# Average pooling over 2x2x2 windows: all loads contiguous and, but for the first, paired, twelve of them for ten, and two stores for three

## The chip, the cores and the metric

One core of one Trainium2 chip. The time is the device time of one execution in microseconds (us). A KB is 1024 bytes; "a load of 24 KB" has 24 KB in each of 128 partitions, so 3 MiB.

## The reference

```python
x: (8, 32, 32, 32, 32) float32, kernel_size = 2
result[:, :, i, j, k] = mean(x[:, :, 2*i:2*i+2, 2*j:2*j+2, 2*k:2*k+2])   # (8, 32, 16, 16, 16)
```

It reads 32 MiB and writes 4 MiB. The 256 pairs of batch and channel are 256 rows of 128 KB. Any piece that holds whole pairs of planes (8 KB a pair) can be pooled by itself, so a partition may take a piece of its own row, or all partitions together one contiguous stretch.

## The kernel before

The first half of the input is read with one row per partition, pieces 128 KB apart; the second half in contiguous stretches.

```python
KF = 256                                   # 1 KB of float32
xv = x.rearrange("b c d h w -> (b c) (d h w)")[:P]              # first half
xf = x.rearrange("b c d h w -> (b c d h w)")[P * 128 * KF:]     # second half
plan = [(0, 0, 32), (0, 32, 32), (0, 64, 32), (0, 96, 32),
        (1, 0, 24), (1, 24, 24), (1, 48, 24), (1, 72, 24), (1, 96, 16), (1, 112, 16)]
for t, k, kb in plan:
    tin = pool_in.tile([P, 32 * KF], F32, tag="tin", name="tin")      # 5 buffers
    buf = tin[:, :kb * KF]
    src = xv[:, k*KF:(k+kb)*KF] if t == 0 else xf[P*k*KF:P*(k+kb)*KF].rearrange("(p e) -> p e", p=P)
    nc.sync.dma_start(out=buf, in_=src)
    pool_unit(buf, t, k, kb, split=k == 96 and t == 1)   # add planes, add columns, add rows and scale
# stores: contiguous part 1 (3 KB runs), the whole first half (16 KB runs), contiguous part 2 (2 KB runs)
... (cut) ...
# on the built program: a contiguous load reads two rows at once
elif "in_" in src.memref and ap[0][0] == row:
    ap = [[2 * row, 64], [1, 2 * row]]
... (cut) ...
# the first load is moved ahead of the opening barrier; the end waits for the stores alone
```

Per unit the vector engine (DVE) makes two adds and a third that also scales; each of the three counts one on its semaphore. All transfers are issued by the queue of SyncE (SPq).

## Time and profile before

| | before |
|---|---|
| time, median | 91.38 us (91.28 to 91.54, 6 runs) |
| span of the profile | 86.7 us |
| DMA queue's share of 16 engines | 99.2% |
| DVE busy | 64.5 us |
| loads land (from vector starts and issues) | 12.0, then every 9.7, 7.30 and 4.9; the last at 80.1 |
| last store lands | 89.9 us |

The lines that carry this are shown in the prediction. Each is read for its releaser: a vector instruction that waited for a transfer starts as that transfer lands.

### The profile page before, as it was taken

The numbers are of one execution on the slowest core, as the hardware profiler recorded it, in microseconds if no ns is written. First come the engines' busy times: TensorE is split into PE (matmuls) and PEld (weight loads), VectorE is DVE, ScalarE is ACT, GpSimd is POOL, SyncE is SP. The second block draws the span as 40 slices with busy tenths as digits, with TensorE's granted clock in tenths as the row PEclk, the third lists the DMA queues.
The fourth block names the chain that finished last, engine by engine and source line by source line (L and its number), as shares of the span: only waits on it lengthen the run. The fifth ranks groups of instructions, "written<-read, shape, count | busy, mean of one in ns | idle before, by whom it ended". The sixth has DMA issues, their size and how long they took to land.

```text
span 86.7 us, 91 instructions
## 1 busy us (share of the span) xinstructions
DVE 64.5 (74%) x41; POOL 0.2 (0%) x4
## 2 busy tenths in 40 slices
DVE  0000049992999649992999999799599959999992
POOL 0000000000000000000000000000000000000000
DMA  8969998899988999699888988889988899889999
GB/s 242 469 287 454 484 484 378 363 469 484 484 363 363 484 484 484 287 439 605 363 363 386 703 363 363 363 363 658 431 363 363 363 484 484 363 363 424 414 463 401
DMA packets 1297, 36.72 MB, mean 424 GB/s; under 512 B 176, under 2 KB 176, under 8 KB 176
## 3 DMA queue, kind: packets, MB, share of 16 engines
q1 hardware_dynamic: 1297, 36.72, 99.2%
HBM read 33.55 MB, written 4.19 MB: 436 GB/s over the span
## 4 chain that ended last, share of the span: by engine, by line
DMA 70%; DVE 26%; issue 0%; SPq 0%; DVEq 0%
DMA tin<-in_x_dram 70%; DVE tin L68 14%; DVE tin L71 8%; DVE obuf L74 4%; SPq L87 0%; DVE dummy L74 0%; DVEq L105 0%
## 5 line engine op out<-in xcount | busy, mean ns | idle before, releaser
L68 DVE TENSOR_TENSOR tin<-tin 128x4096 f32<-128x4096 f32 (+3 forms) x11 | 35.9, 3260 | 19.9 <-DMA tin<-in_x_dram 19.9
L71 DVE TENSOR_TENSOR tin<-tin 128x2048 f32<-128x2048 f32 (+2 forms) x10 | 18.6, 1865 | 0.3
L74 DVE CUSTOM_DVE_ANT_1 obuf<-tin 128x1024 f32<-128x1024 f32 (+2 forms) x10 | 10.1, 1011 | 0.3
L74 DVE DVE_READ_ACCUMULATOR2_ANT dummy<- 128x1 f32 x10 | 0.8, 82 | 0.0
L210 POOL MEMSET const-bfloat16-1.0<- 128x1 bf16 x1 | 0.1, 102 | 0.0
L210 POOL MEMSET const-uint8-127<- 128x1 uint8 x1 | 0.1, 102 | 0.0
L210 POOL MEMSET const-float32-0.0<- 128x1 f32 x1 | 0.1, 99 | 0.2 <-issue 0.2
L210 POOL MEMSET const-float32-1.0<- 128x1 f32 x1 | 0.1, 99 | 0.0
## 6 DMA issues: line engine op xcount, KB each, us to landing
tin<-in_x_dram SPq DMA_DIRECT2D x4, 4096.0 KB, 25.5
tin<-in_x_dram SPq DMA_DIRECT2D x4, 3072.0 KB, 34.5
tin<-in_x_dram SPq DMA_DIRECT2D x2, 2048.0 KB, 25.5
out_dram<-obuf SPq DMA_DIRECT2D x1, 2048.0 KB, 10.3
out_dram<-obuf SPq DMA_DIRECT2D x1, 1536.0 KB, 6.2
out_dram<-obuf SPq DMA_DIRECT2D x1, 512.0 KB, 4.8
```

Source lines behind the costliest of these rows:

```text
L68: nc.vector.tensor_add(out=bv[:, o0:o1], in0=a[:, o0:o1, 0], in1=a[:, o0:o1, 1])
L71: nc.vector.tensor_add(out=c, in0=bv[:, :, 0], in1=bv[:, :, 1])
L74: nc.vector.tensor_tensor_reduce(out=obuf[t][:, o0:o0 + od * 256].rearrange("p (j k) -> p j k", k=16), in0=cv[:, :, 0], in1=cv[:, :, 1], s ...
L210: nc = _bacc.Bacc("TRN2", target_bir_lowering=False, num_devices=1)
```

## The change

Its intent: one uniform layout, with every load contiguous and, from the second on, paired, that is, read as 64 rows of double length; sizes that let the vector engine keep up; two stores instead of three, of which the first is held until shortly before the loads end.

```diff
-    pool_in = ... bufs=5          # of 32 KB
+    pool_in = ... bufs=6          # of 24 KB
-    plan = [(0, 0, 32), ... (1, 112, 16)]
+    plan = [24] * 8 + [16] * 4
-        src = xv[...] if t == 0 else xf[...]
+        nc.sync.dma_start(out=buf, in_=xf[P*k*KF:P*(k+kb)*KF].rearrange("(p e) -> p e", p=P))
-    for k, n, kb in [(0, 4, 3), (12, 2, 2)]: ... and the whole first half after the first
+    for k, n, kb in [(0, 8, 3), (24, 4, 2)]:
...
+    plain = next(i for i in program if isinstance(i, mybir.InstDMACopy))    # the first load stays unpaired
-        elif "in_" in src.memref and ap[0][0] == row:
+        elif "in_" in src.memref:
             ap = [[2 * row, 64], [1, 2 * row]]
...
-        copy.replace(w, wait_value=w.wait_value + 1) if w.ant_name.startswith("DVE") else w
+        copy.replace(w, wait_value=31) if w.ant_name.startswith("DVE") else w
```

More of the change, by code (lines that the diff above doesn't have):

```diff
@@ L27, in pool_rows, with pool_unit @@
     add = mybir.AluOpType.add
-    xv = x.rearrange("b c d h w -> (b c) (d h w)")[:P]
-    ov = out.rearrange("b c d h w -> (b c) (d h w)")[:P]
-    xf = x.rearrange("b c d h w -> (b c d h w)")[P * 128 * KF:]
-    of = out.rearrange("b c d h w -> (b c d h w)")[P * 16 * KF:]
-    pool_in = ctx.enter_context(tc.tile_pool(name="pin", bufs=5))
+    xf = x.rearrange("b c d h w -> (b c d h w)")
+    of = out.rearrange("b c d h w -> (b c d h w)")
+    pool_in = ctx.enter_context(tc.tile_pool(name="pin", bufs=6))
     pool_out = ctx.enter_context(tc.tile_pool(name="pout", bufs=1))
-    obuf = [pool_out.tile([P, 16 * KF], F32, name=f"obuf{t}") for t in range(2)]
+    obuf = pool_out.tile([P, 32 * KF], F32, name="obuf")
     dummy = pool_out.tile([P, 1], F32, name="dummy")
-    plan = [
-        (0, 0, 32),
-        (0, 32, 32),
-        (0, 64, 32),
-        (0, 96, 32),
-        (1, 0, 24),
-        (1, 24, 24),
-        (1, 48, 24),
-        (1, 72, 24),
-        (1, 96, 16),
-        (1, 112, 16),
-    ]
-    def pool_unit(buf, t, k0, kb, split):
+    plan = [24] * 8 + [16] * 4
+    def pool_unit(buf, k0, kb):
         od = kb // 8
@@ L64, in pool_unit @@
         b = buf[:, :od * 1024]
-        bv = b.rearrange("p (o e) -> p o e", o=od)
-        cuts = (0, 1, od) if split else (0, od)
-        for o0, o1 in zip(cuts, cuts[1:]):
-            nc.vector.tensor_add(out=bv[:, o0:o1], in0=a[:, o0:o1, 0], in1=a[:, o0:o1, 1])
+        nc.vector.tensor_add(
+            out=b.rearrange("p (o e) -> p o e", o=od), in0=a[:, :, 0], in1=a[:, :, 1])
         bv = b.rearrange("p (e ww) -> p e ww", ww=2)
@@ L74, in pool_unit @@
         nc.vector.tensor_tensor_reduce(
-            out=obuf[t][:, o0:o0 + od * 256].rearrange("p (j k) -> p j k", k=16),
+            out=obuf[:, o0:o0 + od * 256].rearrange("p (j k) -> p j k", k=16),
             in0=cv[:, :, 0], in1=cv[:, :, 1],
@@ L78, in pool_unit @@
         )
-    for t, k, kb in plan:
-        tin = pool_in.tile([P, 32 * KF], F32, tag="tin", name="tin")
+    k = 0
+    for kb in plan:
+        tin = pool_in.tile([P, 24 * KF], F32, tag="tin", name="tin")
         buf = tin[:, :kb * KF]
-        if t == 0:
-            src = xv[:, k * KF:(k + kb) * KF]
-        else:
-            src = xf[P * k * KF:P * (k + kb) * KF].rearrange("(p e) -> p e", p=P)
-        nc.sync.dma_start(out=buf, in_=src)
-        pool_unit(buf, t, k, kb, split=k == 96 and t == 1)
-    for k, n, kb in [(0, 4, 3), (12, 2, 2)]:
+        nc.sync.dma_start(
+            out=buf, in_=xf[P * k * KF:P * (k + kb) * KF].rearrange("(p e) -> p e", p=P))
+        pool_unit(buf, k, kb)
+        k += kb
+    for k, n, kb in [(0, 8, 3), (24, 4, 2)]:
         nc.sync.dma_start(
             out=of[P * k * KF:P * (k + n * kb) * KF].rearrange("(u p e) -> p u e", u=n, p=P),
-            in_=obuf[1][:, k * KF:(k + n * kb) * KF].rearrange("p (u e) -> p u e", u=n),
+            in_=obuf[:, k * KF:(k + n * kb) * KF].rearrange("p (u e) -> p u e", u=n),
         )
-        if k == 0:
-            nc.sync.dma_start(out=ov, in_=obuf[0])
 def kernel(tc: tile.TileContext, x: bass.AP, kernel_size: int, out: bass.AP):
@@ L107 @@
     program = blocks[tc.starting_block_idx].instructions
+    plain = next(i for i in program if isinstance(i, mybir.InstDMACopy))
     for n, i in enumerate(program):
-        if not isinstance(i, mybir.InstDMACopy):
+        if not isinstance(i, mybir.InstDMACopy) or i is plain:
             continue
```

## The prediction

> **What bounds the kernel now.** I read the page's head, then the DMA queue line, then the timeline of the vector engine (DVE) and of the queue that issues transfers (SPq), and last the chain, because here the chain misleads.
>
> ```profile
> span 86.7 us, 91 instructions
> DVE 64.5 (74%) x41; POOL 0.2 (0%) x4
> ...
> q1 hardware_dynamic: 1297, 36.72, 99.2%
> HBM read 33.55 MB, written 4.19 MB: 436 GB/s over the span
> ...
> DMA 70%; DVE 26%; issue 0%; SPq 0%; DVEq 0%
> ...
> out_dram<-obuf SPq DMA_DIRECT2D x1, 2048.0 KB, 10.3
> out_dram<-obuf SPq DMA_DIRECT2D x1, 1536.0 KB, 6.2
> out_dram<-obuf SPq DMA_DIRECT2D x1, 512.0 KB, 4.8
> ```
>
> The packets of one queue fill 99.2% of sixteen transfer engines' span: they are never without work. The vector engine is busy 74% and has its rests. The chain gives it 26% all the same, because the span ends with the last instruction, the issue of the last store at 85.11, and not with that store's landing; before that issue stands the vector work on the last load. But the landing is what the time waits for. From the next view, the three stores were issued at 77.66, 78.33 and 85.11; with the medians above they landed at 77.66 + 6.2 = 83.9, 78.33 + 10.3 = 88.6 and 85.11 + 4.8 = 89.9. So the last store was in the queue 3.5 us before the one ahead of it was through. The end is 89.9 in the trace's clock, and the time of 91.35 is 1.45 more, outside what the trace shows; I carry it over unchanged.
>
> ```profile
> 12.01 4.42 DVE L68 TENSOR_TENSOR tin<-tin 128x4096 f32<-128x4096 f32 x1 [12.01 <-DMA tin<-in_x_dram]
> ...
> 21.70 4.42 DVE L68 TENSOR_TENSOR tin<-tin 128x4096 f32<-128x4096 f32 x1 [1.67 <-DMA tin<-in_x_dram]
> ...
> 31.42 4.43 DVE L68 TENSOR_TENSOR tin<-tin 128x4096 f32<-128x4096 f32 x1 [1.71 <-DMA tin<-in_x_dram]
> ...
> 55.74 3.36 DVE L68 TENSOR_TENSOR tin<-tin 128x3072 f32<-128x3072 f32 x1 [0.53 <-DMA tin<-in_x_dram]
> ...
> 63.04 3.36 DVE L68 TENSOR_TENSOR tin<-tin 128x3072 f32<-128x3072 f32 x1 [1.15 <-DMA tin<-in_x_dram]
> ...
> 70.34 3.36 DVE L68 TENSOR_TENSOR tin<-tin 128x3072 f32<-128x3072 f32 x1 [1.15 <-DMA tin<-in_x_dram]
> ...
> 76.41 2.48 DVE L68 TENSOR_TENSOR tin<-tin 128x1024 f32<-128x1024 f32 x2
> 77.66 0.62 SPq L93 DMA_DIRECT2D out_dram<-obuf  x1
> 78.33 0.58 SPq L98 DMA_DIRECT2D out_dram<-obuf  x1
> ...
> 85.11 0.57 SPq L93 DMA_DIRECT2D out_dram<-obuf  x1
> ```
>
> A row that ends with a DMA as releaser starts as its load lands, so these starts are a clock of the loads. Loads of 32 KB a partition (4 MiB, one row read at a time, rows of the tensor 128 KB apart) land every 9.7 us; loads of 24 KB (3 MiB, contiguous, two rows in one read) every 7.30. The two 16 KB loads were issued at 49.17 and 55.24 and took 26.0 and 24.9 to land: at 75.2 and 80.1, so 4.9 each. The steps are 9.71 - 7.30 = 2.41 and 7.30 - 4.90 = 2.40: **a load costs 0.08 us and 2.405 us per MiB**, whether contiguous and paired or neither. The first began 12.01 - 9.71 = 2.30 us after the start. The stores follow the same line: from 80.1 to 89.9 is 9.8 us for 4 MiB in three, and 4 x 2.405 + 3 x 0.08 = 9.86.
>
> **What the Trainium skill says.** "DMA: Bandwidth & Descriptors", Specifications, gives a fabric ceiling of 435 GB/s for the sixteen engines' way into SBUF. The trace agrees: 2.405 us per MiB is 436 GB/s. "HBM Reference", Specifications, says that a core streaming alone measures about 425 GB/s, bounded by its engines; agreed, 4.194 MB in 9.71 us is 432. The same DMA page, Latency and other measured facts, reports that a row pitch of 512 KiB or more lowers the rate (207 GB/s at 512 KiB). The old first half has a pitch of 128 KiB, which the page doesn't list, and its loads ran at 432 GB/s against 431 for the contiguous ones: there is no such loss to win back here. And its Queues, rings and completion order says that an engine consumes descriptors in ring order; agreed: the first store was issued at 77.66 yet landed 3.8 us after the last load, about what its own bytes take (1.5 x 2.405 = 3.6).
>
> **The change, part by part.**
>
> Loads. Bytes are the same, 32 MiB. Four of 32, four of 24 and two of 16 KB become eight of 24 and four of 16. Old sum: 2.30 + 4 x 9.71 + 4 x 7.30 + 2 x 4.90 = 80.14, which the trace confirms (80.1). New: 2.30 + 8 x 7.30 + 4 x 4.90 = 80.30. That is +0.16, two more loads at 0.08. Contiguity and pairing get nothing, since the two kinds already lie on one line. The first load stays unpaired and comes before the opening barrier as before, so the 2.30 stays.
>
> Buffers. Six of 24 KB in place of five, mixed. Load 7 waits for unit 1 to be worked off, at about 9.6 + 6.1 = 15.7, while five loads still queue behind unit 1 until 2.30 + 6 x 7.30 = 46.1. The last load waits for unit 6, at about 46.1 + 6.1 = 52.2, and its turn comes at 75.4. The queue stays fed.
>
> Vector work. A 24 KB unit takes 76.41 - 70.34 = 6.07 us, a 16 KB unit 4.20 (80.80 to 85.00 in the timeline). Twelve units: 8 x 6.07 + 4 x 4.20 = 65.4 busy against 64.5. All of it lies beside transfers, as 6.07 < 7.30 and 4.20 < 4.90. Near the end: unit 8 lands at 2.30 + 58.4 = 60.7 and is done at 66.8; unit 9 runs to 71.0, unit 10 to 75.2; unit 11 lands at 75.4, its first add (2.29 us) ends at 77.7; unit 12 lands at 80.3 and is done at 84.5.
>
> First store, 24 KB a partition (3 MiB). It now waits for vector count 31. Each unit counts three; the old wait of 24 + 1 was for the first add of unit 9, which the trace confirms (77.66 is where the first of the two short adds from 76.41 ends). So 31 is the first add of unit 11, 77.7: 2.6 us ahead of the loads' end, against 80.1 - 77.66 = 2.4 before, where the engines didn't run dry. It moves from 80.3 to about 80.30 + 3 x 2.405 + 0.08 = 87.6.
>
> Second store, 8 KB (1 MiB). Issued at about 84.5, still 3.1 us before the one ahead of it is through; of these the issue takes 0.6 and the way to the first byte about 1.2 (the chain shows the first load's transfer from 1.18 after its issue at 0). So it hides. Both stores: 4 x 2.405 + 2 x 0.08 = 9.78; the same sum lay 0.06 above the old measurement, so 9.7 to 9.8. Two MiB now go out in runs of 2 and 3 KB in place of 16 KB; the old store with 3 KB runs kept the line (3.8 measured, 3.7 by the sum), so I charge nothing.
>
> Sum: 80.30 + 9.75 = 90.05, and 1.45 after it: **91.5 us**, +0.15 on 91.35.
>
> **The rivals.**
> 1. Contiguous, paired reads are faster, and the half that gets them pays. For it: longer reads mean fewer packets. Against: 7.30 lies on the line through 9.71 and 4.90 to 0.01 us. Even 1% on 16 MiB would be 0.4 us: 91.1.
> 2. The second store becomes a new wait. One long store behind one short one leaves fewer transfers in the queue. If the last store missed its place by 1 us the time were 92.5. Against: 3.1 us of lead, and the store ahead of it is 3 MiB rather than 2.
> 3. The first store leaves a hole at 80.3. It has 8 runs a partition to describe, in place of 4; issues took 0.62 us with four and 0.57 with two, so some 0.73 with eight. A lead of 2.6 should take that; if not, some tenths.
> 4. Short runs to memory are slow. If the 2 MiB that move from 16 KB runs to 2 and 3 KB lost 5%, that were 0.24 us: 91.75.
>
> **Range and chances.** The sum of small terms is +0.15. Repeats spread by 0.11 us; rivals 3 and 4 could add 0.3, rival 1 take 0.3 away. So 91.5, with 91.15 to 91.95. For 2% either way the time must reach 89.5 or 93.2. The first needs an end at 88.1, which is less than the bytes take at the shown rate (2.30 + 36 x 2.405 = 88.9); the second needs a hole of 1.7 us, which only rival 2 or 3 in full could make.
>
> **What the changed profile would show.** Loads landing every 7.30 and then 4.90 us, the last at 80.3, say that the line holds; 7.2 or less would be rival 1. The first store issued at 77.7 and landing at 87.6 says that it kept its place; a later landing is rival 3 or 4. The second issued near 84.5 and landing at 90.0. DVE near 65.4. The span should fall to about 86.1, as the last issue comes 0.6 earlier, though the time does not: the chain will still name vector work that decides nothing. The prediction is wrong if the DMA share falls well below 99%, or if the time outside the trace isn't 1.45 again.

## The result, and the profile after

| | before | after |
|---|---|---|
| time, median | 91.38 us (91.28 to 91.54) | 92.27 us (92.09 to 92.45), 6 runs each |
| ratio | | 1.0097, 95% interval 1.0080 to 1.0114 |

Ratios are the mean time of one kernel's fast runs over that of the other's of the same rounds, so not quite the ratio of the medians. The change costs 0.9 us: within 2%, but six times the 0.15 us forecast, and outside the range.

From the page of the changed kernel: head, DMA queue, chain, and the stores' issues with their us to landing.

```profile
span 86.9 us, 100 instructions
DVE 65.4 (75%) x48; POOL 0.2 (0%) x4
...
q1 hardware_dynamic: 1151, 36.68, 99.0%
...
DMA 82%; DVE 12%; SPq 3%; issue 0%; DVEq 0%
...
out_dram<-obuf SPq DMA_DIRECT2D x1, 3072.0 KB, 10.0
out_dram<-obuf SPq DMA_DIRECT2D x1, 1024.0 KB, 5.5
```

The vector engine's time is what the sum said, 65.4. The queue's share looks healthy. The timeline of the changed kernel shows where the time went:

```profile
10.39 3.36 DVE L50 TENSOR_TENSOR tin<-tin 128x3072 f32<-128x3072 f32 x1 [10.39 <-DMA tin<-in_x_dram]
...
17.68 3.36 DVE L50 TENSOR_TENSOR tin<-tin 128x3072 f32<-128x3072 f32 x1 [1.13 <-DMA tin<-in_x_dram]
...
61.51 3.36 DVE L50 TENSOR_TENSOR tin<-tin 128x3072 f32<-128x3072 f32 x1 [1.15 <-DMA tin<-in_x_dram]
...
78.51 7.43 SPq L75 DMA_DIRECT2D out_dram<-obuf  x2
...
81.06 2.29 DVE L50 TENSOR_TENSOR tin<-tin 128x2048 f32<-128x2048 f32 x1 [0.59 <-DMA tin<-in_x_dram]
```

The first load lands at 10.39 where 9.60 was forecast. From there all is as forecast: 7.29 to the second, (61.51 - 17.68) / 6 = 7.305 for each of the next six, and (81.06 - 61.51) / 4 = 4.89 for each of the last four. The loads end at 81.06 rather than 80.30; the delay of the first 10 us is carried to the end.

**What the completion records add.** The Trainium skill, "DMA: Bandwidth & Descriptors", Why a DMA increments its semaphore by 16 and not by 1, says that each transfer engine adds one when its own share has landed. The trace agrees: every load has sixteen marks, and the load is usable at the last. So one can see how even the engines are. The median mark is here the ninth of the sixteen:

```
                         last mark   median mark   last minus median
before, first load         11.99        11.86            0.13
before, last load          80.11        79.97            0.14
after,  first load         10.37         9.54            0.83
after,  last load          81.04        80.22            0.82
```

Before, a load of 24 KB in first place would have had its median mark at 11.86 - 2.41 = 9.45; after, it is at 9.54. So most engines are nearly as early as before and **one is far behind** (the second-last mark is at 9.92). A packet is what one engine reads at once, here one row of the load. The packet records show the late one: the sixteen first packets (32 KB) of the kernel before end between 2.80 and 3.18 us; those of the changed one (24 KB) end between 2.38 and 3.20, but for one that took 2.38 us, where the median took 1.59, and ended at 3.65. After that its packets take 0.91 to 0.93 as all others do. The marks of the first and the last load show the same distance: no load makes the lag up. In the last store it is still 0.63.

In the profiled runs (92.31 against 91.29) the last store lands at 90.92 against 89.90, and the time outside the trace is 1.39 in both. The 1.02 divides into the first load, 10.37 - (11.99 - 2.41) = 0.79; the other loads, (81.04 - 10.37) - (80.11 - 11.99 + 2.405) = 0.15; and the stores, (90.92 - 81.04) - (89.90 - 80.11) = 9.88 - 9.79 = 0.09.

### The profile page after: what moved, and what is told of

Read it like the earlier page. It is cut to its first block, busy times and chain, and to the rows that moved or that the text cites. A ratio compares the mean times of both kernels' runs of the same rounds, so it can differ in the third digit from the quotient of the medians.

```text
span 86.9 us, 100 instructions
## 1 busy us (share of the span) xinstructions
DVE 65.4 (75%) x48; POOL 0.2 (0%) x4
## 4 chain that ended last, share of the span: by engine, by line
DMA 82%; DVE 12%; SPq 3%; issue 0%; DVEq 0%
DMA tin<-in_x_dram 82%; DVE tin L50 7%; DVE tin L54 3%; SPq L67 3%; DVE obuf L57 2%; DVE dummy L57 0%; DVEq L85 0%
## 5 line engine op out<-in xcount | busy, mean ns | idle before, releaser
L50 DVE TENSOR_TENSOR tin<-tin 128x3072 f32<-128x3072 f32 (+1 forms) x12 | 36.0, 3002 | 19.2 <-DMA tin<-in_x_dram 19.0
L54 DVE TENSOR_TENSOR tin<-tin 128x1536 f32<-128x1536 f32 (+1 forms) x12 | 19.0, 1580 | 0.4
L57 DVE CUSTOM_DVE_ANT_1 obuf<-tin 128x768 f32<-128x768 f32 (+1 forms) x12 | 10.4, 869 | 0.4
```

The source lines that it names most:

```text
L50: nc.vector.tensor_add(out=b.rearrange("p (o e) -> p o e", o=od), in0=a[:, :, 0], in1=a[:, :, 1])
L54: nc.vector.tensor_add(out=c, in0=bv[:, :, 0], in1=bv[:, :, 1])
L57: nc.vector.tensor_tensor_reduce(out=obuf[:, o0:o0 + od * 256].rearrange("p (j k) -> p j k", k=16), in0=cv[:, :, 0], in1=cv[:, :, 1], scal ...
```

## The experiments

Each was timed beside the kernel before. "Lag" is the last mark of the first load less the median mark. It and the landings are of the one profiled run of each kernel; the times are of four to six runs. Eighteen kernels were run, in five groups.

### Group 1: pairing, the form of the issue, or the sizes?

The first theory was that the paired loads queued in the first 2 us, which take longer to issue, hold up an engine's first packet. The rivals: the first load's size, or its contiguous layout.

**Six loads unpaired.** `plain` holds the first six loads instead of one:

```diff
-    plain = next(i for i in program if isinstance(i, mybir.InstDMACopy))
+    plain = [i for i in program if isinstance(i, mybir.InstDMACopy)][:6]
```

> The changed kernel with its first six loads (those issued at the start) reading one row at a time, as only its first did; loads 7 to 12 stay paired. Theory P (the paired loads that are issued in the first 2 us hold up one engine's first packet, and that engine stays behind to the end): the first load lands at about 9.6 instead of 10.37, the landing spread of its 16 engines falls from 1.2 to about 0.35 us, the time is about 91.5. Theory S (a first load of 24 KB rows starts worse than one of 32 KB): still 10.3 and 92.3. Theory C (the contiguous layout of the first load starts worse than the 128 KB pitch): still 10.3 and 92.3.

Measured: 92.18 us, ratio 1.0090 (1.0075 to 1.0105), first landing 10.17, lag 0.61.

**All twelve unpaired** (`[:12]`).

> The changed kernel with all twelve loads reading one row at a time. Theory P: as the run with six plain loads, 91.5; should pairing of the later loads be worth something, that run is the faster of the two. Theories S and C: 92.3.

Measured: 92.28 us, ratio 1.0088 (1.0076 to 1.0100), first landing 10.37, lag 0.83. The theory falls: with no pairing anywhere the loss is whole. Nor is pairing worth anything later.

**Six unpaired, but with the long issue form** (the same, and for loads 2 to 6 also `ant_dge_precooked=False`).

> As the run with six plain loads, but loads 2 to 6 take the longer issue (without the sequencer's short form, which the paired ones also lack; some 0.56 us an issue instead of 0.33 to 0.47). If theory P holds because of the issue form and not of the pairing: 92.3 and a first landing at 10.3. If because of the paired reads themselves: 91.5 and 9.6.

Measured: 92.18 us, ratio 1.0086 (1.0073 to 1.0099), first landing 10.10, lag 0.49. The form of the issue does nothing either.

**Old sizes, contiguous.** `plan = [32] * 4 + [24] * 4 + [16] * 2`, five buffers of 32 KB, four unpaired loads, the split add of the kernel before and three stores (runs of 3, 4 and 2 KB, where that kernel had 3, 16 and 2).

> The changed kernel's contiguous layout with the load sizes of the kernel before (four of 32, four of 24, two of 16 KB), its first four loads unpaired, the others paired as before, its split first add and its three stores. Theory P and theory S: first load lands at 12.0 as before, time 91.4. Theory C: it lands near 12.8, time 92.2.

Measured: 91.60 us, ratio 1.0026 (1.0012 to 1.0039), first landing 12.26, lag 0.32. Most of the loss is gone with 32 KB, though all is contiguous; the lag is still over twice the 0.13 of the kernel before. At this point size looked like the cause.

### Group 2: size of the first load, or distance between its rows?

**First load of 32 KB, then eight of 24 and two of 16**, contiguous, in a buffer of its own; three stores.

> Pairing is out: with all loads unpaired the first load still landed at 10.37. The changed kernel with a first load of 32 KB rows (contiguous, unpaired), then eight of 24 and two of 16 KB, a split add and three stores. Theory F (the rows of the very first load alone decide how far the slowest engine falls behind): first landing 12.0 to 12.3 as with the old sizes, last engine at most 0.35 us after the median one, time 91.5 to 91.7. Theory Q (that the queue behind it is made of 24 KB rows, or holds six loads, decides): last engine 0.5 to 0.8 us after the median, first landing 12.5 to 12.8, time 92.0 to 92.3.

Measured: 91.73 us, ratio 1.0044 (1.0031 to 1.0057), first landing 12.27, lag 0.25. The first load decides most of it, not the queue behind it.

**First load of 16 KB** (`[16] + [24] * 8 + [16] * 3`), in a buffer of its own; three stores.

> The same with a first load of 16 KB rows, eight of 24, three of 16 KB. Theory F with size as cause (shorter first rows leave the slowest engine further behind): last engine over 0.8 us behind the median one, time 92.3 to 92.7. If only rows that are not a power of two (24 KB) are bad: last engine at most 0.35 us behind, time 91.6 to 91.8.

Measured: 92.24 us, ratio 1.0103 (1.0088 to 1.0118), first landing 8.01, lag 0.68. That lag lies between the two expectations; the time is just short of the size theory's range.

**The kernel before with 24 KB rows.** The first half in 24, 24, 24, 24 and 32 KB, still 128 KB apart:

```diff
-        (0, 0, 32), (0, 32, 32), (0, 64, 32), (0, 96, 32),
+        (0, 0, 24), (0, 24, 24), (0, 48, 24), (0, 72, 24), (0, 96, 32),
```

> The kernel before with its first half read in four loads of 24 KB and one of 32 KB a partition, rows still 128 KB apart: one more load, 0.08 us. Size as cause: last engine 0.5 to 0.8 us behind the median, first landing 10.1 to 10.4, time 92.0 to 92.3. Pitch between the rows as cause (the contiguous layout is what hurts): last engine 0.15 to 0.3 behind, first landing 9.6 to 9.75, time 91.5.

Measured: 91.36 us, ratio 1.0000 (0.9988 to 1.0012), first landing 9.62, lag 0.17. Its timeline, beside that of the changed kernel above:

```profile
9.64 3.36 DVE L69 TENSOR_TENSOR tin<-tin 128x3072 f32<-128x3072 f32 x1 [9.64 <-DMA tin<-in_x_dram]
...
16.92 3.36 DVE L69 TENSOR_TENSOR tin<-tin 128x3072 f32<-128x3072 f32 x1 [1.13 <-DMA tin<-in_x_dram]
```

Loads of the same size as the changed kernel's land 0.75 earlier, and the time is that of the kernel before. **So size is not the cause.** Where the rows lie remains; group 3 tests it on the first load alone.

**First load paired too**, so that it reads 48 KB at once (`or i is plain` taken out).

> The changed kernel with its first load paired too, so that the first packets read 48 KB. Size of the first packet as cause: last engine at most 0.3 us behind the median; the longer issue costs up to 0.2 us; time 91.6 to 91.8. Layout as cause: 0.5 to 0.8 behind, time 92.3 to 92.5.

Measured: 92.43 us, ratio 1.0128 (1.0110 to 1.0145), first landing 10.47, lag 0.45. The longer issue starts its packets at 1.36 instead of 1.02, and the lag stays high, though just under the 0.5 that was expected of the layout: longer packets don't mend it.

### Group 3: the first load alone, and a version to beat both

Here the first load takes its rows from elsewhere, so a part of the result is wrong on purpose. Bytes, sizes, order and stores stay.

**Changed kernel, first load's rows 128 KB apart:**

```diff
-            out=buf, in_=xf[P * k * KF:P * (k + kb) * KF].rearrange("(p e) -> p e", p=P))
+            out=buf, in_=(
+                xf[:P * 128 * KF].rearrange("(p e) -> p e", p=P)[:, :kb * KF] if k == 0 else
+                xf[P * k * KF:P * (k + kb) * KF].rearrange("(p e) -> p e", p=P)))
```

> The changed kernel, but its first load alone takes its 24 KB rows 128 KB apart instead of back to back (results wrong on purpose in that part; bytes, sizes and all else as they are). Theory C1 (the layout of the very first load decides how far the slowest engine is left behind): last engine 0.1 to 0.3 us behind the median one, first landing 9.6 to 9.75, time 91.5 to 91.6. Rival (the contiguous loads queued behind it matter too): 0.5 or more behind, time 92.0 or more.

Measured: 91.63 us, ratio 1.0025 (1.0013 to 1.0037), lag 0.12.

```profile
9.57 3.36 DVE L50 TENSOR_TENSOR tin<-tin 128x3072 f32<-128x3072 f32 x1 [9.57 <-DMA tin<-in_x_dram]
...
80.25 2.29 DVE L50 TENSOR_TENSOR tin<-tin 128x2048 f32<-128x2048 f32 x1 [0.60 <-DMA tin<-in_x_dram]
```

This one edit brings the first landing to 9.57 and the last to 80.25; the forecast had 9.60 and 80.30. In ratios it takes back 1.0097 - 1.0025 = 0.72%, about 0.66 of the 0.89 us. What stays is 0.25% or 0.23 us (0.12 to 0.34). It is of the size of the 0.15 that was forecast, but not all of that kind: in the profiled runs the loads end 80.23 - 80.11 = 0.12 later than in the kernel before, and the stores take 90.23 - 80.23 = 10.00 for its 9.79.

**Rows 48 KB apart** (48 for 128 in that edit).

> The same with rows 48 KB apart (results wrong on purpose). If the lag falls steadily with the distance (back to back 24 KB: 0.5 to 0.8; 32 KB: 0.25 to 0.3; 128 KB: 0.15): last engine 0.2 to 0.3 behind, time 91.6 to 91.8. If only a wide or a power-of-two distance helps: 0.5 or more, time 92.0 or more.

Measured: 92.32 us, ratio 1.0099 (1.0086 to 1.0112), first landing 10.38, lag 0.74. Twice the distance, no gain at all: the lag doesn't fall steadily.

**Kernel before, first load's 32 KB rows back to back** (and kept unpaired).

> The kernel before, but its first load alone takes its 32 KB rows back to back (results wrong on purpose in that part). Theory C1: last engine 0.25 to 0.35 behind the median one as in the two runs with a contiguous 32 KB first load, first landing 12.2 to 12.3, time 91.5 to 91.7. Rival (contiguous loads behind the first matter): 0.13 behind as before, time 91.35.

Measured: 91.62 us, ratio 1.0019 (1.0007 to 1.0030), first landing 12.21, lag 0.33. The reverse test: contiguous rows in the first load alone cost the kernel before 0.2 us.

**Eight loads, all rows 128 KB apart** (48, 48, 32, 40, 32, 24, 16, 16 KB; three stores; correct).

> A version that should beat both: all rows 128 KB apart, eight loads of 48, 48, 32, 40, 32, 24, 16, 16 KB instead of ten, three stores, correct results. Two loads fewer at 0.08 us: 91.2, ratio 0.998, if the last engine stays within 0.2 us of the median one. If lag grows with size or a store comes late: 91.4 or more.

Measured: 92.11 us (91.93 to 93.15), ratio 1.0093 (1.0056 to 1.0130), lag 0.43. A miss. In the profiled run, one of the longer ones (92.81), beside the lag, the last load lands 81.66 - 75.46 = 6.2 us after the one ahead of it instead of 4.9; packets of 16 KB that take 0.61 elsewhere took up to 1.68 there. Its first store had been issued at 71.79, while the loads still ran.

### Group 4: which distance, and the version again

**Rows of 24 KB, 32 KB apart.**

> The changed kernel with the 24 KB rows of its first load alone 32 KB apart (results wrong on purpose). Theory T (a distance that is a power of two keeps the sixteen engines even): last engine 0.15 to 0.35 us behind the median one, time 91.6 to 91.8. Theory W (only a wide distance does): 0.5 or more behind, time 92.1 or more.

Measured: 91.77 us, ratio 1.0047 (1.0034 to 1.0061), lag 0.20.

**64 KB apart.**

> The same, 64 KB apart (results wrong on purpose). Theory T: 0.1 to 0.3 behind, 91.6 to 91.7. Theory W, with the limit somewhere above 48 KB: anything between 91.6 and 92.2, worse than at 120 KB.

Measured: 91.57 us, ratio 1.0024 (1.0010 to 1.0039), lag 0.13.

**120 KB apart.**

> The same, 120 KB apart (results wrong on purpose). Theory T: 0.5 or more behind, 92.1 or more. Theory W: 0.1 to 0.3 behind, 91.6 to 91.7.

Measured: 92.35 us, ratio 1.0111 (1.0098 to 1.0124), lag 0.81. The first landings of the last two, 64 KB and then 120 KB:

```profile
9.61 3.36 DVE L50 TENSOR_TENSOR tin<-tin 128x3072 f32<-128x3072 f32 x1 [9.61 <-DMA tin<-in_x_dram]
```

```profile
10.45 3.36 DVE L50 TENSOR_TENSOR tin<-tin 128x3072 f32<-128x3072 f32 x1 [10.45 <-DMA tin<-in_x_dram]
```

Width is out: 120 KB is as bad as 24, while 32 is nearly good.

**Eight loads, first of 32 KB, first store held.** Loads of 32, 48, 48, 40, 32, 24, 16, 16 KB, stores reordered so that the first was issued only at 77.96.

> All rows 128 KB apart, loads of 32, 48, 48, 40, 32, 24, 16, 16 KB, the first store issued only at about 77.4. If the early store slowed the last load of the version before: last load's landing 4.9 after the one ahead, time 91.2, ratio 0.998. If strided 16 KB rows themselves do it: again over 5.5 between the last two landings, time 91.8 or more.

Measured: 91.23 us median, ratio 1.0014 (0.9980 to 1.0048). Four of six runs took 91.12 to 91.25, two 92.01 and 92.08. The profile caught one of the longer two:

```profile
12.13 4.42 DVE L66 TENSOR_TENSOR tin<-tin 128x4096 f32<-128x4096 f32 x1 [12.13 <-DMA tin<-in_x_dram]
...
26.64 6.56 DVE L66 TENSOR_TENSOR tin<-tin 128x6144 f32<-128x6144 f32 x1 [6.50 <-DMA tin<-in_x_dram]
...
41.54 6.56 DVE L66 TENSOR_TENSOR tin<-tin 128x6144 f32<-128x6144 f32 x1 [3.14 <-DMA tin<-in_x_dram]
...
54.03 5.49 DVE L66 TENSOR_TENSOR tin<-tin 128x5120 f32<-128x5120 f32 x1 [0.74 <-DMA tin<-in_x_dram]
```

The first 48 KB load took 14.51, the second, of the same form, 14.90; the 40 KB load took 12.49 where 0.08 + 5 x 2.405 = 12.11. Its last load took 4.89, so the slow last load of the version before is gone; but as the start was changed along with the store, and slow loads came elsewhere, it is not shown that the early store had caused it. In four runs of six the version is below every run of the kernel before (91.26 to 91.49); by the ratio it is not established as faster.

### Group 5: a power of two, or a multiple of 32 KB?

**96 KB apart.**

> The changed kernel with the 24 KB rows of its first load alone 96 KB apart (results wrong on purpose). Power of two as the rule: last engine 0.5 or more behind the median one, 92.1 or more. Multiple of 32 KB as the rule: 0.1 to 0.3 behind, 91.55 to 91.8.

Measured: 91.75 us, ratio 1.0043 (1.0022 to 1.0063), first landing 9.88, lag 0.50.

**160 KB apart.**

> The same, 160 KB apart (results wrong on purpose). Power of two: 0.5 or more behind, 92.1 or more. Multiple of 32 KB: 0.1 to 0.3 behind, 91.55 to 91.8. If 96 and 160 differ, neither rule holds.

Measured: 91.66 us, ratio 1.0031 (1.0006 to 1.0055), first landing 9.73, lag 0.26.

All distances for 24 KB rows in the first load of the changed kernel together, against the kernel before:

| distance, KB | 24 | 48 | 120 | 32 | 64 | 96 | 128 | 160 |
|---|---|---|---|---|---|---|---|---|
| ratio | 1.0097 | 1.0099 | 1.0111 | 1.0047 | 1.0024 | 1.0043 | 1.0025 | 1.0031 |
| first landing, us | 10.37 | 10.38 | 10.43 | 9.70 | 9.59 | 9.88 | 9.55 | 9.73 |
| lag, us | 0.83 | 0.74 | 0.81 | 0.20 | 0.13 | 0.50 | 0.12 | 0.26 |
| longest first packet, us | 2.38 | 2.50 | 2.08 | 1.85 | 1.70 | 1.75 | 1.73 | 1.73 |

By the times the multiples of 32 KB stand apart from the others, and 96 and 160 KB rule out that only powers of two do well. The lag of 0.50 at 96 KB is above what was expected; its time is within. The last row, read from the packet records, parts the two groups too, and there 96 KB stands with the other multiples: its one late engine read for 1.75, about the longest at 128 KB (1.73), but began only at 1.42. Nor is the lag alone what a kernel pays: the run with six loads unpaired and the long issue form had a lag of 0.49, about that of 96 KB, but a first landing of 10.10 for 9.88, and took 92.18 us for 91.75. Among the kernels whose first load has 24 KB rows, the ratios follow the first landing more closely than the lag.

So the rule fits the times, with a shade between the multiples. Two limits: the three bad distances are all multiples of the row, 24 KB (so is 96, which is good), and no others were tried; and 96 and 160 KB ran on another chip than 32, 48, 64, 120 and 128, and no bad distance was run beside them there.

## Why the prediction was wrong

**The step that failed** is this one: "Contiguity and pairing get nothing, since the two kinds already lie on one line. The first load stays unpaired and comes before the opening barrier as before, so the 2.30 stays." The line was right, and it holds between landings. The 2.30 was taken as a constant of the start, though it had been measured once, on a load whose rows lie 128 KB apart. In the changed kernel it is 10.37 - 7.30 = 3.07. Of the 0.77 between them, 0.45 is one engine of sixteen whose first packet ends that much after the next to last; the rest is that the next to last is late as well (9.92). In other kernels with back-to-back rows it is several: with the long issue form the last two marks are both at 10.10. Since the sixteen marks keep their distances to the last load, the delay is carried whole to the end of the loads. That the first load's layout causes it is shown by one edit: putting the first load's rows 128 KB apart takes back 0.66 us of the 0.89.

Point by point:
- **Cost of a load, 0.08 us and 2.405 us per MiB: right.** 7.305 and 4.89 measured for 7.30 and 4.90. The two more loads cost 0.15 for the 0.16 forecast, by the landings.
- **Contiguity and pairing: right in steady flow, wrong for the start.** Runs with six or all loads unpaired had ratios of 1.0090 and 1.0088. Rival 1 thought of contiguity as a gain; it turned out to be a loss, and only in the first load.
- **Buffers and vector work: right.** 65.4 us busy; no load came late for want of a buffer.
- **First store: right in kind.** It was issued at 78.51, later than the forecast 77.7 by what the loads were late, and landed at 78.51 + 10.0 = 88.5.
- **Second store: right.** Its issue ended at 78.51 + 7.43 = 85.94 and took 0.56, so it began at 85.38, 3.1 us before the first was through. It landed at 85.38 + 5.5 = 90.9. Rivals 2 and 3 didn't come. One reading was wrong without harm: the 1.18 taken from the chain is where the issue of the third load began, not where the first load's transfer did; its packets start at 1.01.
- **Stores' own time: mis-sized by 0.1.** 9.7 to 9.8 was forecast, 9.88 measured in the changed kernel. From the last load's landing to the last store's, the five kernels that write half of the output or more in runs of at least 12 KB took 9.75 to 9.80, the fifteen that write runs of 2 to 4 KB took 9.82 to 10.00. That is rival 4, in the changed kernel at under half of the 0.24 it was given: it fits, though no experiment changed the runs to memory alone.
- **Span: wrong with the start.** 86.9 for 86.1, since the last issue came at 85.38 and not at 84.5.
- **"The prediction is wrong if the DMA share falls well below 99%": a bad guard.** It was 99.0%. One engine that is late by half a microsecond is 0.5 / 16 / 86.9 = 0.04% of the share. The other guard held: the time outside the trace was 1.39 in both profiled runs. (The prediction's 1.45 took the median time, 91.35, with the end of a run of 91.29.)
- **The row pitch: read too strongly.** The 207 GB/s that the prediction cites at 512 KiB is for copies between HBM tensors, per direction, and the same row of the Trainium skill's page gives 214 as the full rate of these. It is not to be set against the 432 of these loads, so it says little of what a pitch would cost here.

**What stays open.** Why multiples of 32 KB keep the first packets short: the trace shows when packets end, not what they meet in memory. Nor is the distance all. Back to back, rows of 32 KB (a multiple) left lags of 0.25 to 0.33, and rows of 48 KB, 128 KB apart, one of 0.43. The last version's first load, the same as that of the kernel before, had a lag of 0.30 for its 0.13 in a run of 92.01 us, so lags of that size also differ without a cause that was found. Rows of 16 KB back to back had 0.68, which fits the rule, in one kernel. Open too is what slows single loads of the versions with eight large loads.

## What to carry to other kernels

In a kernel bound by its transfers, read the start apart from the steady rate: here what the last engine lost in its first packet was not won back by eleven more loads. Take the first load's rows in an arrangement that was measured, and when the layout of the first load changes, treat the time to its landing as unknown. Look at the marks of the single engines, as a share that is averaged over sixteen doesn't show one or a few that are late.

## What the Trainium skill lacked or had wrong

- "DMA: Bandwidth & Descriptors", Latency and other measured facts, warns only of large powers of two between rows (512 KiB and more, in copies between HBM tensors). Here 32, 64 and 128 KB between rows of the first load gave ratios of 1.0024 to 1.0047, and 24, 48 and 120 KB gave 1.0097 to 1.0111: at the start it was the other distances that cost time. In steady flow 128 KB apart ran at 432 GB/s, no slower than contiguous.
- No page was found that has the unevenness of the start. "DMA: Bandwidth & Descriptors" knows engines that are slower for other reasons, and that a bulk load runs at the pace of its slowest engine, but not a lag that arises in the first packet alone: the lag of the last engine behind the median one, 0.12 to 0.83 us in the first load, stays to the last load (0.83 and 0.82 in the first and last load of the changed kernel).
- "SBUF — State Buffer", The DMA setup-cost knee, gives each transfer a fixed cost of about 2 us. For loads queued behind one another the runs show 0.08 us; only the first shows a cost of that order, 2.30 in the kernel before.
